# Later weight reloads, float32r filter taps and idle-time transposes at the start of a hybrid encoder block

## The chip, the cores and the metric

The kernel runs on one NeuronCore of a Trainium2 chip. The metric is the device time of one execution in microseconds. The engines are named as the profile names them: PE (matrix multiply) with its weight loads PEld, DVE (VectorE), ACT (ScalarE), POOL (GpSimd) and SP (the queue that issues nearly all DMAs). Each engine runs its own list of instructions in order and waits on semaphores for the others.

## What is computed

One layer of an encoder block, width 2048, 512 tokens, float32 inputs and outputs. Cut to what matters here:

```python
def reference(x, c, w_ada, b_ada, w_in, b_in, ...):
    cond = jax.nn.silu(c)
    mod = (cond @ w_ada[l] + b_ada[l])[:, None, :]
    sh1, sc1, g1, sh2, sc2, g2 = jnp.split(mod, 6, axis=-1)
    h = x * (1.0 + sc1) + sh1
    z = h @ w_in[l] + b_in[l]
    z_u, z_v, z_h, z_g = jnp.split(z, split_pts, axis=-1)
    y_a = spatial_gating(gelu(z_u), gelu(z_v), ...) @ w_branch_a[l]
    y_b = hyena(z_h, ...) @ w_branch_b[l]
    mix = (gate_a * y_a + gate_b * y_b) @ w_o[l] + b_o[l]
    x = layer_norm(ALPHA * x + g1 * mix, ...)
    h = x * (1.0 + sc2) + sh2
    x = layer_norm(ALPHA * x + g2 * (relu(h @ w_m1 + b_m1) ** 2 @ w_m2 + b_m2), ...)

def hyena_filters(L, w1, b1, w2, b2, freq, w3):
    h = jnp.sin(fr * (feats @ w1 + b1))
    h = jnp.sin(fr * (h @ w2 + b2))
    h = h @ w3
    return h.reshape(L, HY_DIRS, HY_ORDER, HY_WIDTH) * window
```

`hyena` convolves its value stream twice with filters of length 512 on both sides; the kernel does this with discrete transforms as matrix products.

## The kernel before

Dense products are made of float32r parts. `split` makes of a float32 tile a high part (an ACT cast, `hi`) and a low part (a DVE subtraction, `lo`); a product is three passes: high by high, high by low, low by high. `dense_steps` makes a group: 512 output columns of one weight matrix for all 512 tokens, in `kp` steps of two input tiles `kc`, with four PSUM banks. One `kp` of a group is 24 matmuls of 128x512 and one weight block.

Weight blocks (128x1024, 512 KB) go through rings of three buffers: `wraw` (as loaded), `whi` and `wlo` (split). The class `Weights` keeps them going: `load` issues the DMA of the next block; `prepare` takes loaded blocks, splits them and calls `load` for each, as long as no more than `ahead` split blocks are waiting; `take`, called by a group, calls `prepare` and hands out a split block. The order of all this is the order in which the program is written: every engine's list and the SP queue follow it.

The start has three parts that matter here.

- **Opening.** Features, `cond` and first modulation tiles are loaded. `Sine` (L283 to L292) runs the filter network: a matmul, a range reduction on DVE, a sine on ACT, twice. The second sine gives the taps' stationary operand in two forms, `even` and `odd` (L361, L362), read with a stride of four.
- **Filter stage.** Eight rounds `n`. A round makes four tap products (`taps`, L385, float32, two passes each) for the next round, one transform of this round's windowed taps (`Forward`, L319 to L331, six float32 products), two modulation sums (`ada_steps(2)`), the window products on DVE (L395) and the transform's sums on DVE (L335 to L339, six operations). Spectra are stored to DRAM.
- **Value groups.** Two dense groups (`two`) run side by side, one `kp` step of each in turn, while the modulated input they read is still being made. An input tile `kc` needs four modulation sums on DVE (L261, `scalar_tensor_tensor` of a 512 KB tile `araw` with `cond`), two small sums on POOL (`mod`, L267, L268), two ACT operations (`act`, L426, and `xT`, L427) and a subtraction on POOL (L428). `ada_steps(4)` does one `kc`. Five `kc` are made in the filter stage; eleven in this stage, at the places that the loop `for kp in range(8)` gives: `weights.prepare()` first, then `ada_steps(4)` until `2 * kp + 2 + LEAD` tiles are there (`LEAD` is 3), then the two groups.

Modulation tiles have three buffers of their own and, while the input tiles are few, up to eight more of the input tiles' own room (`Modulation.load`); a tile is loaded when a sum has freed one. `weights.load()` is called three times at rounds 4 to 6, the first `prepare` at round 6.

After the value groups come about 2550 us of dense groups that this change leaves as they are.

Of the kernel before, what the change touches and what calls it, by code (L numbers as in the profile page):

```python
# [13 lines left out]
AF = mybir.ActivationFunctionType  # L14
# [26 lines left out]
def block_kernel(ctx: ExitStack, tc: tile.TileContext, t):  # L41
# [12 lines left out]
    def slot(name, dt=F32):  # L54
        return heap.tile([P, 512], dt, name=name, tag="slot")

    def slot_pair(name):
        return slot(name + "h", F32R), slot(name + "l", F32R)
# [5 lines left out]
    def bank(name):  # L64
        return psum.tile([P, 512], F32, name=name, tag="bank")

    def f32(ap):
        return ap.bitcast(F32)

    def load(dst, src, queue=nc.sync):  # L70
        queue.dma_start(dst, src)
        return dst

    def split(src, hi, lo):

        nc.scalar.copy(hi, src)  # L76
        nc.vector.tensor_tensor(lo, src, f32(hi), op=OP.subtract)  # L77
# [34 lines left out]
    class Weights:  # L112


        def __init__(self):
            self.blocks = blocks()
            self.raw, self.ready, self.kept, self.used = [], [], {}, set()
            self.ahead, self.done = 1, False

        def load(self):  # L120
            w, cg, kp = next(self.blocks, (None, 0, 0))
# [18 lines left out]
        def prepare(self):  # L140
            for _ in range(4):
                if not self.raw:
                    return
                ring = sum(not self.keeps(r[2]) for r in self.ready)
                if ring > self.ahead and not self.keeps(self.raw[0][1]):
                    return
                raw, what = self.raw.pop(0)
                hi, lo = self.tiles(what)
                split(raw, hi, lo)
                self.ready.append((hi, lo, what))  # L150
                self.load()

        def take(self, w, cg, kp):
            if (w.name, cg, kp) in self.used:
# [58 lines left out]
    def cload(name, shape, queue=nc.sync):  # L213
        return load(const.tile(list(shape), F32, name="c_" + name), t[name], queue)
# [1 line left out]
    warm = small.tile([P, 1], F32, name="warm", tag="warm")  # L216
    nc.vector.memset(warm, 0.0)
    nc.scalar.activation(warm, warm, AF.Sigmoid)
    hw1 = cload("hw1", (EMB, HID), nc.scalar)
    featT = load(slot("featT")[:EMB], t["featT"], nc.scalar)  # L220
    hcol = cload("hcol", (P, 3), nc.scalar)
    hw2 = cload("hw2", (HID, P), nc.scalar)
    cond = const.tile([P, D], F32, name="cond")
    for h in range(4):
        c_ = slice(512 * h, 512 * (h + 1))
        load(cond[:, c_], t["c"][:, c_].broadcast_to([P, 512]))
    inv_d = const.tile([P, 1], F32, name="inv_d")
    nc.vector.memset(inv_d, 1.0 / D)
    sign = const.tile([P, 1], F32, name="sign")
# [4 lines left out]
    nc.gpsimd.memset(first_tap[:, 0:1], 1.0)  # L234
    ident = const.tile([P, P], F32, name="ident")
    make_identity(nc, ident)


    dots = const.tile([P, 6, KC, 2], F32, name="dots")
# [2 lines left out]
    class Modulation:  # L242
# [16 lines left out]
        def step(self):  # L259
            _, raw, m, kc, h = self.raw.pop(0)  # L260
            nc.vector.scalar_tensor_tensor(raw, raw, 1.0, cond[:, 1024 * h:1024 * (h + 1)], op0=OP.mult,  # L261
                                           op1=OP.mult, accum_out=dots[:, m, kc, h:h + 1])
            if len(self.raw) < 10:
                self.load()

    def mod_sum(m, kc, eng=nc.vector):
# [36 lines left out]
    class Forward:  # L303
# [30 lines left out]
        def sums(self, tiles):  # L334
            nc.vector.tensor_tensor(self.ea, self.e0, self.eo, op=OP.add)  # L335
            self.minus(self.e0, self.e0, self.eo)
            for half, e in enumerate((self.ea, self.e0)):
                o = self.o[half]
                nc.vector.tensor_tensor(tiles[half], e, o, op=OP.add)  # L339
                self.minus(tiles[2 + half], e, o)  # L340
# [4 lines left out]
    class Filters:  # L345


        def __init__(self):
            self.one = Sine(hw1, featT, 0, HID)
            self.src, self.raw, self.stores, self.kept, self.win, self.ps = [], [], [], {}, [], []  # L350

        def middle(self):
            x = self.one.reduce()
# [3 lines left out]
        def ready(self):  # L357

            x = self.two.reduce()
            even, odd = slot("a2"), slot("a2")  # L360
            nc.scalar.activation(even, x, AF.Sin)  # L361
            nc.scalar.activation(odd, x, AF.Sin, scale=sign)  # L362
            self.a2 = [a.rearrange("h (p k) -> h k p", k=4) for a in (even, odd)]

        def fetch(self, n):

# [5 lines left out]
            if n in (0, 2):  # L372
                for i in (2, 3) if hf else (0, 1):
                    self.win.append(load(actp.tile([P, 1024], F32, name="win", tag="act"), t["win"][i]))

        def taps(self, n):

            cs = PARTS[n][2]
            if cs == 0:
                self.w = self.raw.pop(0)  # L380
            w, skip = self.w
            for cl in range(4):
                ps = bank("flt")
                extra = cs == 0 and cl == 0
                nc.tensor.matmul(ps, self.a2[cs][:, cl, :], w, start=True, stop=not extra)  # L385
                if extra:
                    nc.tensor.matmul(ps, first_tap, skip, start=False, stop=True)
                self.ps.append(ps)
# [66 lines left out]
    quarters = [cond[:, 512 * h:512 * (h + 1)] for h in range(4)]  # L455
    for s_, c_ in zip(silu, quarters):
        nc.scalar.activation(s_, c_, AF.Sigmoid)
    flt.middle()
    for s_, c_ in zip(silu, quarters):
        nc.vector.tensor_tensor(c_, c_, s_, op=OP.mult)  # L460
# [3 lines left out]
    def x_load():  # L464
        if len(xt) < KC:
            xt.append(load(slot("xT"), t["xT"][len(xt)]))
# [3 lines left out]
    def ada_steps(n):  # L470

        for _ in range(n):
            ada.step()
            done.append(None)
            if len(done) % 4 == 0:
                first_input(len(h1), xt[len(h1)])
                x_load()
# [2 lines left out]
    ada.load()  # L480
    fc = table("fwd", 3)
    for m in (1, 4):
        nc.gpsimd.tensor_scalar(bada[:, m], bada[:, m], 1.0, None, op0=OP.add)
    ada_steps(2)
    flt.ready()
    x_load()
    for _ in range(5):
        ada.load()
    flt.taps(0)
    ada_steps(2)  # L490
    flt.windowed(0)
    for n in range(8):
        if n < 6 and n % 2 == 0:
            flt.fetch(n + 2)
        if n < 7:
            flt.taps(n + 1)
        sums = flt.transform(n)
        ada_steps(2)
        if n < 7:
            flt.windowed(n + 1)  # L500
            flt.store()
        sums()
        if 4 <= n < 7:
            weights.load()
        if n == 6:
            weights.prepare()
    flt.win = []
    windows.clear()
# [3 lines left out]
    two = [dense_steps(ps, t["w_in"], 4 + i, 8, h1) for i, ps in enumerate(ps_v)]  # L512
    yv = []
    for kp in range(8):
        weights.prepare()
        while len(h1) < min(KC, 2 * kp + 2 + LEAD):
            ada_steps(4)
        for i, group in enumerate(two):
            next(group)
            if kp == 7:  # L520
                next(group, None)
                yv.append(short_conv(ps_v[i], 0, i))
        if kp == 1:
            flt.store()
            bin_c = cload("bin", (P, 72))
            hcw = cload("hcw", (P, 24, 4))
            cb = const.tile([P, 24], F32, name="cb")
        if kp == 4:
            nc.vector.tensor_tensor(cb, hcw[:, :, 1], bin_c[:, 16:40], op=OP.mult)
            nc.vector.tensor_tensor(cb, cb, hcw[:, :, 3], op=OP.add)  # L530


    def to_tokens(src, cl, dst):
# [246 lines left out]
    def parts(kc):  # L780
        hi, lo = act_pair(kc)
        split(mix[kc], hi, lo)
        mp.append((hi, lo))
# [343 lines left out]
```

## Time and profile before

| | us |
|---|---|
| median of three runs | 2767.09 |
| lowest, highest run | 2763.63, 2767.69 |
| profiled execution | 2766.04 |
| span of its instructions | 2764.0 |
| PE busy in the span | 2704.5 |
| DVE busy | 1520.6 |
| ACT busy | 770.2 |
| POOL busy | 109.6 |
| mean granted PE clock | 0.992 of full speed |

The span runs from the first to the last instruction; the profiled execution's own time is 2 us longer, for what lies around it. Busy times are sums over the whole span, so they do not say which engine holds a stage up; that is read from single stages. In a timeline a row gives the start, the length, the engine, the line and the operation with its tiles (output, arrow, inputs), how many like it follow each other, and in brackets how long the engine stood idle before it and what ended that. A matmul's record is longer than its distance to the next one, since matmuls overlap; distances are read from starts.

### The profile page before, as it was taken

Reading aid. Unit: us, or ns where it says so; the run is one execution under the profiler, and the core shown is the slowest. Engines: PE = TensorE matmul, PEld = TensorE weight load, DVE = VectorE, ACT = ScalarE, POOL = GpSimd, SP = SyncE. Lnnn points to the kernel's source line nnn. Section 1 sums busy time; section 2 is a strip of 40 time slices with the busy share of each in tenths; the row PEclk is TensorE's granted clock in tenths of the full one; section 3 lists DMA queues with packets and bytes.
Section 4 is the critical chain, followed back from the end, with each engine's and each line's share of the span. In section 5 each row is a group of like instructions: output and inputs, shape, how many; then the busy total and the mean of one; then the engine's idle time right before and its main releaser. Section 6 shows DMA issues by size and latency. Waiting matters only on the chain.

```text
span 2764.0 us, 29765 instructions
## 1 busy us (share of the span) xinstructions
PE 2704.5 (98%) x11917; PEld 2201.6 (80%) x11917; DVE 1520.6 (55%) x2027; ACT 770.2 (28%) x934; POOL 109.6 (4%) x103
## 2 busy tenths in 40 slices
PE   7989999999999999999999999999999999999996
PEld 3667777888888888887988888888888888888885
DVE  7866968644566657536774343343433433434348
ACT  2234322322222222314631221312213122131232
POOL 1120000000000000040020000000000000000001
PEclk9989999999999999999999999999999999999998
DMA  8672332555665558454452323233223233223342
GB/s 328 240 291 77 124 105 99 190 192 190 200 210 191 185 197 294 136 186 163 166 164 96 99 92 102 96 99 97 94 99 97 94 99 100 94 91 105 98 141 74
DMA packets 120474, 400.46 MB, mean 145 GB/s; under 512 B 14219, under 2 KB 14315, under 8 KB 120208
## 3 DMA queue, kind: packets, MB, share of 16 engines
q1 hardware_dynamic: 120024, 398.46, 42.7%
q8 instruction: 93, 1.52, 0.2%
q14 instruction: 45, 0.37, 0.0%
q10 hardware_dynamic: 312, 0.11, 0.0%
HBM read 388.01 MB, written 10.50 MB: 144 GB/s over the span
## 4 chain that ended last, share of the span: by engine, by line
PE 88%; DVE 4%; DMA 2%; issue 1%; ACT 1%; SPq 0%; POOL 0%; DVEq 0%; ACTq 0%
PE d L187 56%; PE t L872 28%; DMA araw<-in_ada 1%; DVE araw L261 1%; DVE wlo L77 1%; PE inv L626 1%; PE inv L614 0%; DMA wraw<-in_w_m 0%; DVE r L993 0%; DVE r L995 0%; DVE r L888 0%; DVE gated L887 0%; DVE st L890 0%; PE tr L537 0%; PE h2T L912 0%
## 5 line engine op out<-in xcount | busy, mean ns | idle before, releaser
L187 PE MATMUL d<-act,whi 128*128 128x512 f32 (+1 forms) x4224 | 1286.9, 387 | 16.2 <-POOL act L428 9.7
L77 DVE TENSOR_TENSOR wlo<-wraw,whi 128x1024 fp32r<-128x1024 f32 x480 | 589.2, 1231 | 1035.2 <-ACT whi L76 1035.1
L187 PEld LDWEIGHTS d<-act,whi 128*128 128x128 f32 x4224 | 788.0, 189 | 181.8 <-POOL act L428 11.3
L76 ACT CAST whi<-wraw 128x1024 fp32r<-128x1024 f32 x480 | 504.4, 1053 | 1534.9 <-PE d L187 914.8
L187 PE MATMUL d<-act,wlo 128*128 128x512 f32 (+1 forms) x2112 | 812.8, 385 | 1.1 <-DVE wlo L77 1.1
L187 PEld LDWEIGHTS d<-act,wlo 128*128 128x128 f32 x2112 | 399.3, 189 | 81.4 <-DVE wlo L77 3.0
L872 PE MATMUL t<-whi,fh 128*128 128x512 f32 x960 | 373.4, 389 | 0.0
L872 PE MATMUL t<-wlo,fh 128*128 128x512 f32 x960 | 373.4, 389 | 0.0
L872 PE MATMUL t<-whi,fl 128*128 128x512 f32 x960 | 373.4, 389 | 0.0
L261 DVE SCALAR_TENSOR_TENSOR araw<-araw,cond 128x1024 f32<-128x1024 f32 x192 | 231.2, 1223 | 9.6 <-DMA araw<-in_ada 9.3
L872 PEld LDWEIGHTS t<-whi,fl 128*128 128x128 f32 x960 | 180.2, 188 | 37.5
L872 PEld LDWEIGHTS t<-whi,fh 128*128 128x128 f32 x960 | 180.2, 188 | 37.4
L872 PEld LDWEIGHTS t<-wlo,fh 128*128 128x128 f32 x960 | 180.2, 188 | 37.4
L872 PE MATMUL t<-whi,act 128*128 128x512 f32 x512 | 160.8, 393 | 0.0
L872 PEld LDWEIGHTS t<-whi,act 128*128 128x128 f32 x512 | 96.9, 189 | 20.2
L887 DVE TENSOR_TENSOR gated<-t,cond 128x512 f32<-128x512 f32 x128 | 87.5, 684 | 31.6 <-PE t L872 31.6
L872 PE MATMUL t<-wlo,act 128*128 128x512 f32 x256 | 100.4, 392 | 2.1 <-DVE wlo L77 2.1
L888 DVE TENSOR_TENSOR r<-r,gated 128x512 f32<-128x512 f32 x128 | 88.6, 692 | 4.4
L187 PE MATMUL d<-whi,act 128*128 128x512 f32 x256 | 78.9, 389 | 0.0
L982 DVE TENSOR_TENSOR relu<-relu 128x512 f32<-128x512 f32 (+1 forms) x68 | 45.6, 671 | 38.2 <-ACT fh L981 38.2
L995 POOL TENSOR_TENSOR r<-r,ln2b 128x512 f32<-128x512 f32 x7 | 11.6, 1662 | 1314.1 <-DVE r L993 1312.8
L872 PEld LDWEIGHTS t<-wlo,act 128*128 128x128 f32 x256 | 48.4, 189 | 12.5 <-DVE wlo L77 2.5
(209 smaller groups left out, 1883.3 us busy)
## 6 DMA issues: line engine op xcount, KB each, us to landing
wraw<-in_w_m SPq DMA_DIRECT2D x264, 512.0 KB, 3.5
araw<-in_ada SPq DMA_DIRECT2D x192, 512.0 KB, 4.9
wraw<-in_w_in SPq DMA_DIRECT2D x144, 512.0 KB, 3.5
wraw<-in_w_o SPq DMA_DIRECT2D x48, 512.0 KB, 3.6
spec<-spec SPq DMA_DIRECT2D x48, 256.0 KB, 3.8
wraw<-in_w_b SPq DMA_DIRECT2D x16, 512.0 KB, 3.5
wraw<-in_w_a SPq DMA_DIRECT2D x16, 512.0 KB, 3.5
xT<-in_xT SPq DMA_DIRECT2D x16, 256.0 KB, 6.4
```

The source lines that it names most:

```text
L76: nc.scalar.copy(hi, src)
L77: nc.vector.tensor_tensor(lo, src, f32(hi), op=OP.subtract)
L187: nc.tensor.matmul(out[i], a, b, start=first and m == 0, stop=last and m == 2)
L261: nc.vector.scalar_tensor_tensor(raw, raw, 1.0, cond[:, 1024 * h:1024 * (h + 1)], op0=OP.mult, op1=OP.mult, accum_out=dots[:, m, kc, h:h + 1])
L626: nc.tensor.matmul(ps[:, cl * P:(cl + 1) * P], conv.y[cl][cs][:, s], ic(4 * cs + COLUMN[cl]), start=(cs == 0), stop=(cs == 1))
L872: nc.tensor.matmul(out[i], a, b, start=kc == 0 and m == 0, stop=kc == 2 * pairs - 1 and m == 2)
L887: nc.vector.tensor_tensor(x, ps[i], g2_row[c], op=OP.mult)
L888: nc.vector.tensor_tensor(r[i][c], r[i][c], x, op=OP.add)
L982: nc.vector.tensor_tensor(x, x, x, op=OP.mult)
L995: eng.tensor_tensor(x, x, ln2_b[c], op=OP.add)
```

## The change

- `Weights.reload` stands where `prepare` called `load`. From before round 0 until after the value groups (`weights.later` is a list) it only notes the load; `weights.flush()`, at the head of each `kp` step, issues what was noted.
- In the `kp` loop one `ada_steps(4)` now comes ahead of `weights.prepare()`, as long as input tiles are missing. The first `prepare` moves from round 6 to round 7.
- Taps: the second sine is written once, split, and its odd form made by two ACT operations on the parts; `parts(n)` splits each `w3` block; a tap is three float32r matmuls instead of one float32 product.
- `busy(n)` issues `n` transposes of the identity into a PSUM bank that nobody reads: 10 between the sines' products, 14 and 14 before the taps.
- The four small loads of the filter network move from the ACT queue to the head of the SP queue, the four loads of `cond` from SP to ACT. The addition of 1 to `bada` moves from POOL to DVE. `step` may load with ten tiles waiting instead of nine.

```diff
@@ class Weights
+        def reload(self):
+            if self.later is None:
+                self.load()
+            else:
+                self.later.append(self.load)
+
+        def flush(self):
+            while self.later:
+                self.later.pop(0)()
...
                 self.ready.append((hi, lo, what))
-                self.load()
+                self.reload()
...
-    hw1 = cload("hw1", (EMB, HID), nc.scalar)
-    featT = load(slot("featT")[:EMB], t["featT"], nc.scalar)
-    hcol = cload("hcol", (P, 3), nc.scalar)
-    hw2 = cload("hw2", (HID, P), nc.scalar)
+    hw1 = cload("hw1", (EMB, HID))
+    featT = load(slot("featT")[:EMB], t["featT"])
+    hcol = cload("hcol", (P, 3))
+    hw2 = cload("hw2", (HID, P))
...
-        load(cond[:, c_], t["c"][:, c_].broadcast_to([P, 512]))
+        load(cond[:, c_], t["c"][:, c_].broadcast_to([P, 512]), nc.scalar)
...
+    def busy(n):
+        ps = bank("busy")
+        for _ in range(n):
+            nc.tensor.transpose(ps[:, :P], ident, ident)
...
-            if len(self.raw) < 10:
+            if len(self.raw) < 11:
                 self.load()
...
-            even, odd = slot("a2"), slot("a2")
-            nc.scalar.activation(even, x, AF.Sin)
-            nc.scalar.activation(odd, x, AF.Sin, scale=sign)
-            self.a2 = [a.rearrange("h (p k) -> h k p", k=4) for a in (even, odd)]
+            nc.scalar.activation(x, x, AF.Sin)
+            even, odd = slot_pair("a2e"), slot_pair("a2o")
+            split(x, *even)
+            for a, b in zip(even, odd):
+                nc.scalar.activation(b, f32(a), AF.Identity, scale=sign)
+            self.a2 = [[a.rearrange("h (p k) -> h k p", k=4) for a in pair] for pair in (even, odd)]
...
+        def parts(self, n):
+            if PARTS[n][2] == 0:
+                w, skip = self.raw.pop(0)
+                both = slot_pair("w3")
+                split(w, *both)
+                self.w.append((*both, skip))
...
-            w, skip = self.w
+            wh, wl, skip = self.w[0] if cs == 0 else self.w.pop(0)
+            ah, al = self.a2[cs]
...
-                nc.tensor.matmul(ps, self.a2[cs][:, cl, :], w, start=True, stop=not extra)
+                for m, (a, w) in enumerate(((ah, wh), (ah, wl), (al, wh))):
+                    nc.tensor.matmul(ps, a[:, cl, :], w, start=m == 0, stop=m == 2 and not extra)
...
     for s_, c_ in zip(silu, quarters):
         nc.scalar.activation(s_, c_, AF.Sigmoid)
+    busy(10)
     flt.middle()
...
     for m in (1, 4):
-        nc.gpsimd.tensor_scalar(bada[:, m], bada[:, m], 1.0, None, op0=OP.add)
+        nc.vector.tensor_scalar(bada[:, m], bada[:, m], 1.0, None, op0=OP.add)
+    busy(14)
     ada_steps(2)
     flt.ready()
+    flt.parts(0)
+    busy(14)
...
     flt.windowed(0)
+    weights.later = []
     for n in range(8):
...
+        if n < 6:
+            flt.parts(n + 2)
         sums()
         if 4 <= n < 7:
             weights.load()
-        if n == 6:
+        if n == 7:
             weights.prepare()
...
     for kp in range(8):
+        weights.flush()
+        if len(h1) < KC:
+            ada_steps(4)
         weights.prepare()
         while len(h1) < min(KC, 2 * kp + 2 + LEAD):
             ada_steps(4)
...
+    weights.flush()
+    weights.later = None
```

How the order of instructions moves is shown at three places. First DVE from the last sums of the filter stage into the value groups, before (`wlo` is the low part of a weight block, `araw` a modulation tile):

```order
L339 TENSOR_TENSOR spec<-bf_e_626,f_o 128x512
L313 SCALAR_TENSOR_TENSOR spec<-bf_e_626,f_o 128x512
L77 TENSOR_TENSOR wlo<-wraw,whi 128x1024 x3
L261 SCALAR_TENSOR_TENSOR araw,dots<-araw,cond 128x1024 x8
L77 TENSOR_TENSOR wlo<-wraw,whi 128x1024 x2
L261 SCALAR_TENSOR_TENSOR araw,dots<-araw,cond 128x1024 x8
```

and with the change:

```order
L356 TENSOR_TENSOR spec<-bf_e_740,f_o 128x512
L330 SCALAR_TENSOR_TENSOR spec<-bf_e_740,f_o 128x512
L77 TENSOR_TENSOR wlo<-wraw,whi 128x1024 x2
L278 SCALAR_TENSOR_TENSOR araw,dots<-araw,cond 128x1024 x4
L77 TENSOR_TENSOR wlo<-wraw,whi 128x1024 x2
L278 SCALAR_TENSOR_TENSOR araw,dots<-araw,cond 128x1024 x4
L77 TENSOR_TENSOR wlo<-wraw,whi 128x1024 x2
L278 SCALAR_TENSOR_TENSOR araw,dots<-araw,cond 128x1024 x4
L77 TENSOR_TENSOR wlo<-wraw,whi 128x1024
L278 SCALAR_TENSOR_TENSOR araw,dots<-araw,cond 128x1024 x4
L77 TENSOR_TENSOR wlo<-wraw,whi 128x1024
```

Eight sums and two splits in turn have become four sums and, from the fourth turn on, one split. Before, two further splits stood ahead of the last round's sums.

Second ACT at the same place, before (two input tiles, then two casts):

```order
L426 ACTIVATE act_858<-xT,mod 128x512
L427 ACTIVATE xT<-xT,mod 128x512
L426 ACTIVATE act_878<-xT,mod 128x512
L427 ACTIVATE xT<-xT,mod 128x512
L76 CAST whi<-wraw 128x1024 x2
```

and with the change:

```order
L452 ACTIVATE act_978<-xT,mod 128x512
L453 ACTIVATE xT<-xT,mod 128x512
L76 CAST whi<-wraw 128x1024
L452 ACTIVATE act_1002<-xT,mod 128x512
L453 ACTIVATE xT<-xT,mod 128x512
L76 CAST whi<-wraw 128x1024
```

Each cast now stands behind the two operations of one input tile instead of a pair of casts behind those of two.

Third ACT between the second sine's product and the first modulated input tile, before:

```order
L284 ACTIVATE sine<-flt,hfb,c_hcol 128x512
L361 ACTIVATE a_181<-sine 128x512
L362 ACTIVATE a_182<-sine,sign 128x512
L426 ACTIVATE act_214<-xT,mod 128x512
L427 ACTIVATE xT<-xT,mod 128x512
```

and with the change:

```order
L301 ACTIVATE sine<-flt,hfb,c_hcol 128x512
L377 ACTIVATE sine<-sine 128x512
L76 CAST a2eh<-sine 128x512
L381 ACTIVATE a2oh<-a2eh,sign 128x512
L381 ACTIVATE a2ol<-a2el,sign 128x512
L76 CAST w3h<-w_124 128x512
L452 ACTIVATE act_272<-xT,mod 128x512
```

The first tap, which waited for the first of two operations, now waits for the last of five.

## Rows read from the trace of the kernel before

**Rows 1.** Stages: span, busy us (count) by engine, PEclk, DMA share, GB/s.
```profile
20.00:98.00 78.00, 77.76 (x169) 39.40 (x170) 68.14 (x111) 13.58 (x20) 6.68 (x12) 1.00 0.71 263
98.00:213.00 115.00, 100.05 (x384) 78.01 (x383) 82.66 (x123) 41.45 (x51) 30.62 (x36) 0.90 0.78 285
213.00:2764.00 2551.00, 2522.70 (x11364) 2083.43 (x11362) 1357.76 (x1772) 707.70 (x854) 65.94 (x43) 1.00 0.40 134
```

**Rows 2.** Timeline of DVE, value groups: the splits of two turns.
```profile
124.45 2.62 DVE L77 TENSOR_TENSOR wlo<-wraw,whi 128x1024 fp32r<-128x1024 f32 x2 [4.25 <-ACT whi L76]
...
140.45 2.61 DVE L77 TENSOR_TENSOR wlo<-wraw,whi 128x1024 fp32r<-128x1024 f32 x2 [4.22 <-ACT whi L76]
```

**Rows 3.** Timeline of the last input tile's turn, all engines.
```profile
192.62 1.21 DVE L261 SCALAR_TENSOR_TENSOR araw<-araw,cond 128x1024 f32<-128x1024 f32 x1
...
193.76 1.22 DVE L261 SCALAR_TENSOR_TENSOR araw<-araw,cond 128x1024 f32<-128x1024 f32 x1
...
198.79 1.23 DVE L261 SCALAR_TENSOR_TENSOR araw<-araw,cond 128x1024 f32<-128x1024 f32 x1 [2.66 <-DMA araw<-in_ada]
...
200.11 0.20 POOL L267 TENSOR_TENSOR mod<-dots 128x2 f32<-128x2 f32 x1 [9.63 <-DVE araw L261]
...
202.18 1.98 ACT L76 CAST whi<-wraw 128x1024 fp32r<-128x1024 f32 x2
...
203.25 1.46 DVE L77 TENSOR_TENSOR wlo<-wraw,whi 128x1024 fp32r<-128x1024 f32 x1 [3.22 <-ACT whi L76]
...
203.68 0.50 PE L187 MATMUL d<-act,whi 128*128 128x512 f32 x1 [1.70 <-POOL act L428]
```

**Rows 4.** Timeline of PE, value groups without waits.
```profile
108.06 0.62 PE L187 MATMUL d<-act,whi 128*128 128x512 f32 x2
...
112.14 0.62 PE L187 MATMUL d<-act,whi 128*128 128x512 f32 x2
```

**Rows 5.** Stretches of the start, columns as in rows 1.
```profile
80.00:97.00 17.00, 17.00 (x41) 8.38 (x41) 15.54 (x24) 5.17 (x7) 1.27 (x1) 1.00 0.03 7
...
205.00:210.00 5.00, 5.00 (x17) 3.95 (x16) 4.89 (x7) 5.00 (x9) 0.00 (x0) 0.67 0.59 210
```

**Rows 6.** Timeline of PE, filter stage: one transform matmul two rounds apart, one round's taps.
```profile
41.89 1.02 PE L319 MATMUL f_ee<-flt,fwd 128*128 128x512 f32 x2
...
47.04 3.60 PE L385 MATMUL flt<-w,a 128*128 128x512 f32 x8
...
60.43 1.02 PE L319 MATMUL f_ee<-flt,fwd 128*128 128x512 f32 x2
```

**Rows 7.** Weight loads by line and form: count, busy us, mean ns, idle before.
```profile
L187 PEld LDWEIGHTS d<-act,whi 128*128 128x128 f32 x4224 | 788.0, 189 | 181.8 <-POOL act L428 11.3 <-issue 7.7 <-ACT act L426 6.6
...
L385 PEld LDWEIGHTS flt<-w,a 128*128 128x128 f32 x64 | 19.4, 311 | 20.0 <-ACT a L361 7.6 <-issue 4.8 <-DVE spec L315 2.3
...
L537 PEld LDWEIGHTS tr<-ident,hy 128*128 128x128 f32 x64 | 9.0, 208 | 1.0 <-issue 0.5
```

**Rows 8.** Timeline of PE: transposes of a later stage.
```profile
224.24 1.11 PE L537 MATMUL tr<-ident,hy 128*128 128x128 f32 x8
```

**Rows 9.** Timeline of the opening, PE and ACT.
```profile
5.13 1.93 PE L283 MATMUL flt<-featT,c_hw 33*64 33x512 f32 x2 [5.13 <-DMA featT<-in_featT]
...
19.56 0.63 ACT L361 ACTIVATE a<-sine 128x512 f32<-128x512 f32 x1 [4.57 <-DVE sine L292]
...
20.24 2.09 PE L385 MATMUL flt<-w,a 128*128 128x512 f32 x2 [6.07 <-ACT a L361]
...
24.27 7.83 PE L385 MATMUL flt<-w,a 128*128 128x512 f32 x14
```

**Rows 10.** Timeline of DVE, end of the filter stage and first value step.
```profile
102.38 1.22 DVE L77 TENSOR_TENSOR wlo<-wraw,whi 128x1024 fp32r<-128x1024 f32 x1
...
109.81 1.23 DVE L77 TENSOR_TENSOR wlo<-wraw,whi 128x1024 fp32r<-128x1024 f32 x1 [4.21 <-ACT whi L76]
110.95 1.22 DVE L261 SCALAR_TENSOR_TENSOR araw<-araw,cond 128x1024 f32<-128x1024 f32 x1
```

More of the change, by code (lines that the diff above doesn't have):

```diff
@@ L117, in __init__ @@
             self.raw, self.ready, self.kept, self.used = [], [], {}, set()
-            self.ahead, self.done = 1, False
+            self.ahead, self.done, self.later = 1, False, None
+        def reload(self):
[6 more added lines that the diff above has]
+                self.later.pop(0)()
         def load(self):
@@ L349, in __init__ @@
             self.one = Sine(hw1, featT, 0, HID)
-            self.src, self.raw, self.stores, self.kept, self.win, self.ps = [], [], [], {}, [], []
+            self.src, self.raw, self.stores, self.kept, self.win, self.ps, self.w = [], [], [], {}, [], [], []
         def middle(self):
@@ L374, in fetch @@
                     self.win.append(load(actp.tile([P, 1024], F32, name="win", tag="act"), t["win"][i]))
+        def parts(self, n):
[4 more added lines that the diff above has]
+                self.w.append((*both, skip))
         def taps(self, n):
             cs = PARTS[n][2]
-            if cs == 0:
-                self.w = self.raw.pop(0)
-            w, skip = self.w
+            wh, wl, skip = self.w[0] if cs == 0 else self.w.pop(0)
+            ah, al = self.a2[cs]
             for cl in range(4):
```

## The prediction

> **What bounds the kernel now.** I read the stages first, then the timelines of single engines, then the waits. In the stage table [rows 1] TensorE (PE) is busy for 2522.7 of the 2551 us after 213 us, and for all of the filter stage (20 to 98). It loses time in one place that this change touches: from 98 to 213 it is busy 100 of 115 us, at a mean granted clock of 0.90. That is the stage of the two value groups. Nothing after it is changed, so the question is when this stage ends.
>
> The stage is not held by PE. VectorE (DVE) runs a loop there: eight modulation sums (two input tiles `kc`), then two low halves of weight blocks (`wlo`), and again. Each time it stands idle for 4.2 us before the first `wlo`, waiting for ScalarE's (ACT's) cast `whi`, and the loop comes back after 140.45 - 124.45 = 16.0 us [rows 2]. ACT itself waits: its queue has the cast behind the two `act` operations of the input tile just summed. One such turn in full [rows 3]: the last sum starts at 198.79, GpSimd's `mod` sum at 200.11, the cast at 202.18, `wlo` at 203.25, that is 4.46 us from the last sum's start to `wlo`. PE needs 10.9 us for the 48 matmuls of a turn (18 of them in 112.14 - 108.06 us, 0.227 each [rows 4]), so it waits, and in such stretches its clock falls to the lower level (0.67 on average from 205 to 210 [rows 5]).
>
> **The filter stage, step by step.** One round of it is four tap products and one transform; the same transform matmul returns after two rounds, at 41.89 and 60.43: 18.54 us a pair [rows 6], all PE. A tap is now two passes of 0.43 us (8 in 3.60, [rows 6]) and becomes three float32r products. Their price is that of the dense loop, 0.227 us, if the strided load of the stationary operand stays hidden: it takes 311 ns where the dense loop's contiguous one takes 189 [rows 7]. Since a matmul can start before the record of its load ends (eight transposes stand in 1.11 us, one every 0.12 [rows 8], with strided loads of 208 ns [rows 7]), I take 0.23. The other end is 311 + 38 = 0.35, the load with the margin that the dense loop leaves (227 - 189). So a round saves 4 x (0.86 - 0.69) = 0.67 and a pair 1.34; at worst a pair costs 4 x (1.05 - 0.86) x 2 = 1.5. DVE gets one more subtraction a pair; it is busy 68 of 78 us in that stage [rows 1], so that is covered. Three pairs follow round 0: **-4.0 us**, bounds -4.4 and +4.5.
>
> The Trainium skill, "TensorE: Matmul & The Clock Gate", section "LDWEIGHTS (loading the stationary operand)", makes the load a matter of columns alone (about 107 ns for 128), whatever the stride. The two load rows [rows 7] differ by 122 ns at equal columns, so the trace speaks against it; by it the load would certainly hide.
>
> Round 0 comes out even. The first product now can start earlier, because the features lead the SP queue instead of the ACT queue beside four loads of `cond`; it waited for them until 5.13 [rows 9]. I take 1 us, between none and 2. But between the second sine and the first tap ACT has four operations more (cast, two sign products, cast of `w3`), near 0.6 us each (the sign product took 0.63 [rows 9]): +2.5, so the first tap moves from 20.24 to 21.7. From there the passes run at the lower clock, 1.03 us each at 20.24, until a little over 27 us (14 passes in 7.83, a mix [rows 9]). Before: 13.4 us of PE work at the high clock (18 tap and 12 transform passes at 0.43, and 0.5 of gaps) from 20.24, half speed to 27.4, gives 37.2. Now 24 x 0.23 + 14 x 0.43 + 0.5 = 12.0 from 22.4 (the low half of `w3` comes last): 36.9. **0**, bounds -2 if the clock were high from the first tap, +2 if it rose one such stretch later. The 38 transposes of `busy` take 0.12 us each at the high clock [rows 8] and 0.24 at the low one, so the 28 ahead of the taps last 6.7 us at most; PE waits 6.07 us for its first tap there [rows 9], and that wait grows by 1.5, so they are free; the ten ahead of the second sine stand in a wait of the same kind. What they can change is the clock. I take no gain from them because near 2 us of idle time remain between the last transpose and the first tap, and an idle time of 1.70 us [rows 3] was followed by the lower level [rows 5].
>
> Here a page speaks against the change: the Trainium skill, "TensorE: Matmul & The Clock Gate", Part 4, says that the high clock does not engage for transposes. No row of this trace shows transposes alone; by the page the sum stays as it is, and if it is wrong here the sum is 2 us better.
>
> **The value groups.** DVE finishes the last transform's sums and two `wlo` at 102.38 [rows 10]. In the change two `wlo` stand behind these sums instead of ahead of them: same count, same moment, less the 4.0: 98.4. PE waits some 3 us there for the first `wlo`; it has slack. Then the difference in order decides. Before, the next thing was a third `wlo`, whose buffer PE freed late, so the first sum started at 110.95 [rows 10]. Now four sums come first, at **98.4**: 12.5 us ahead.
>
> But each `kc` is now followed by its own `wlo`, whose cast stands on ACT behind that `kc`'s `act`. So the idle time comes once per `kc` instead of once per two: three sum pitches of 1.15 (192.62 to 193.76 [rows 3]), 4.46, and 1.14 for the `wlo` (109.81 to 110.95 [rows 10]) make **9.05 us a kc, 18.1 a pair, against 16.0**. From `kc` 5 to `kc` 15 that is ten times 9.05 and two further `wlo` (2.3): 92.8. The last `kc` starts at 191.2, before at 192.62 [rows 3]: the lead is used up. Its last tile is loaded only after its first sum in both kernels, so its `wlo` follows 203.25 - 192.62 = 10.63 later, at 201.8, ready at 203.0.
>
> Now the end. Before, at 203.68 [rows 3], PE had 35 matmuls of the groups left: 7.9 us, and 1.7 lost at the lower clock (0.33 of 5 us [rows 5]): 213.3. Now both blocks of the last step come behind the last `kc`: 48 matmuls, 10.9 us, from 203.0, and the same 1.7: 215.6. **+2.3 us** on the profiled execution, 2766.04 to 2768.3; that execution lies 1.05 under the median of the runs shown, so on the median 2767.09 + 2.3 = **2769.4**.
>
> The reloads themselves cost nothing. SP stood behind `wlo` with a reload whose raw buffer was not yet free, which left the transfers almost idle from 80 to 97 us (share 0.03 [rows 5]); issued a step later they no longer hold the modulation tiles up. But DVE waited for a tile only 2.66 us at the end [rows 3]; the queue was not the bound, so freeing it is worth 0 to 2.7.
>
> **Rivals.**
> - Faster, the loads bind: transfers took 0.78 of the stage [rows 1], after a hole of 17 us [rows 5]. If the loop's 16 us came from them, the groups would run at PE's pace, 16 x 5.45 = 87 us from 97: 184 instead of 213, -29 us, 2738. Against it: DVE's idle rows name the cast, not a tile [rows 2]. 0.04.
> - Faster, the interleaving costs less than I think: 16.0 a pair stays and the lead of 12.5 us remains, less 2.9 for the 13 matmuls that now come behind the last `kc`: -9.6, 2757.5. For it: ACT has nothing else to do. Against it: the cast is queued behind `act`. 0.09.
> - Slower, the clock becomes the bound: PE now works 5.45 us and waits 3.6, again and again, where it waited some 2 us in 16 before. It decides when the lower level lasts through a block: at half the clock a block takes twice 5.45 = 10.9 us, more than the 9.05 of the loop. Priced at the two last blocks low throughout: 21.8 instead of 10.9 + 1.7 = 12.6, so 9.2 beside the 2.3: +11.5, 2778.6. 0.19.
> - Slower, the strided load shows: taps at 0.35 us, +4.5 instead of -4.0, so 8.5 beside the 2.3: +10.8, 2777.9. 0.08.
> - That the change does not move what it says is excluded by the order lists.
>
> **How the numbers follow.** About 0.2% (5.5 us) can be told from no change. The forecast with its own spread (round 0 by 2 either way, the last tile's wait by 2.7 less, the clock by 1.7 either way: 2763 to 2773) has 0.60, nearly all of it inside 0.2%. Faster: 0.04 + 0.09 + 0.02 of the forecast's edge. Slower: 0.19 + 0.08 and 0.02 of its edge. So 0.15, 0.56, 0.29. The range takes in both slower cases and reaches down to 2758: what is left out is the first rival, most of the second, and a clock low for longer.
>
> **What would show it.** In the new profile: pairs of rounds 17.2 us apart; the first modulation sum of the stage near 98.4; DVE idle 3.2 to 3.3 us before nearly every `wlo`, released by `whi`, eleven times; `kc` steps 9.05 apart; PE idle in pieces of 3 to 4 us from about 150 us on; the last `wlo` pair near 203. I am wrong if the `kc` step is well under 9 us, if PE runs without gaps through the stage, or if tap matmuls come slower than one in 0.25 us.

## The result and the profile after

The changed kernel takes 2773.61 us (median of 13 runs, 2770.64 to 2774.97); the kernel before, on the same chips, 2766.13 (median of 13). The ratio is 1.0027, with a 95% interval of 1.0018 to 1.0035: slower by 7.5 us. The range of 2758 to 2779 holds it, but the likeliest case, +2.3 us and hardly to be told from no change, was 5 us too kind. The profiled execution took 2774.97 us, its span 2773.3; it was the slowest of the thirteen, 1.4 us above their median, and the marks below are its own.

First the stages, with the columns of [rows 1]:

```profile
20.00:98.00 78.00, 75.20 (x211) 45.28 (x209) 70.91 (x119) 16.07 (x25) 7.06 (x14) 0.93 0.72 266
98.00:213.00 115.00, 94.43 (x347) 71.85 (x348) 76.42 (x112) 35.06 (x41) 19.71 (x34) 0.89 0.77 275
213.00:2764.00 2551.00, 2531.73 (x11400) 2090.74 (x11398) 1359.15 (x1774) 712.69 (x862) 64.07 (x42) 1.00 0.40 134
```

Between 98 and 213 us TensorE does 347 products instead of 384 [rows 1]. The missing 37 come later; behind them the two kernels run alike.

DVE in the stage of the value groups (start, length, operation, and in brackets the idle time before it and what ended that):

```profile
102.83 1.22 DVE L278 SCALAR_TENSOR_TENSOR araw<-araw,cond 128x1024 f32<-128x1024 f32 x1
...
131.59 1.49 DVE L77 TENSOR_TENSOR wlo<-wraw,whi 128x1024 fp32r<-128x1024 f32 x1 [3.22 <-ACT whi L76]
...
140.88 1.49 DVE L77 TENSOR_TENSOR wlo<-wraw,whi 128x1024 fp32r<-128x1024 f32 x1 [3.22 <-ACT whi L76]
...
198.17 1.21 DVE L278 SCALAR_TENSOR_TENSOR araw<-araw,cond 128x1024 f32<-128x1024 f32 x1
...
204.16 1.23 DVE L278 SCALAR_TENSOR_TENSOR araw<-araw,cond 128x1024 f32<-128x1024 f32 x1 [2.47 <-DMA araw<-in_ada]
...
208.60 3.73 DVE L77 TENSOR_TENSOR wlo<-wraw,whi 128x1024 fp32r<-128x1024 f32 x3 [3.21 <-ACT whi L76]
```

The splits stand 140.88 - 131.59 = 9.29 us apart, one input tile each, with 3.22 us of waiting for the cast in every turn. Over the stage (from 102 to 212 us) that wait adds up as follows in the kernel before (total, times, longest):

```profile
DVE wlo L77 <- ACT whi L76: 28.3, 8, 4.3
```

and in the changed one, in shorter pieces but more of them:

```profile
DVE wlo L77 <- ACT whi L76: 35.4, 11, 3.2
```

One such turn of the changed kernel, ACT, GpSimd, DVE and PE:

```profile
147.53 0.81 ACT L452 ACTIVATE act<-xT,mod 128x512 fp32r<-128x512 f32 x1 [6.68 <-POOL mod L285]
148.38 0.81 ACT L453 ACTIVATE xT<-xT,mod 128x512 f32<-128x512 f32 x1
149.09 1.03 ACT L76 CAST whi<-wraw 128x1024 fp32r<-128x1024 f32 x1
149.26 1.26 POOL L454 TENSOR_TENSOR act<-xT,act 128x512 fp32r<-128x512 f32 x1 [1.77 <-ACT xT L453]
150.16 1.46 DVE L77 TENSOR_TENSOR wlo<-wraw,whi 128x1024 fp32r<-128x1024 f32 x1 [3.21 <-ACT whi L76]
150.18 0.50 PEld L198 LDWEIGHTS d<-act,whi 128*128 128x128 f32 x2 [2.90 <-ACT whi L76]
150.18 1.22 PE L198 MATMUL d<-act,whi 128*128 128x512 f32 x2 [2.48 <-ACT whi L76]
```

The cast needs nothing from this tile: it stands on ACT behind `act` and `xT`, which wait 6.68 us for the sums. TensorE then waits for the cast as well. The split takes 1.46 us instead of 1.22: GpSimd is still busy with L454 when it starts, which the experiments come back to.

The opening on PE, with some of the later `f_ee` rows, which begin a transform (from 44.78 to 62.08 and from 62.08 to 79.40 is a pair of rounds each):

```profile
14.03 2.07 PE L300 MATMUL flt<-sine,c_hw 64*128 64x512 f32 x2 [5.06 <-ACT sine L371]
16.03 5.18 PE L253 MATMUL busy<-ident 128*128 128x128 f32 x28
23.83 0.81 PE L411 MATMUL flt<-w3h,a2eh 128*128 128x512 f32 x1 [2.62 <-ACT w3h L76]
...
35.43 1.02 PE L336 MATMUL f_ee<-flt,fwd 128*128 128x512 f32 x2
...
44.78 1.02 PE L336 MATMUL f_ee<-flt,fwd 128*128 128x512 f32 x2
...
62.08 1.02 PE L336 MATMUL f_ee<-flt,fwd 128*128 128x512 f32 x2
...
70.05 1.02 PE L336 MATMUL f_ee<-flt,fwd 128*128 128x512 f32 x2
...
79.40 1.02 PE L336 MATMUL f_ee<-flt,fwd 128*128 128x512 f32 x2
```

The first tap comes at 23.83 (before 20.24 [rows 9]), the first transform 3.5 us later than before (31.94 there), and a pair of rounds takes 62.08 - 44.78 = 17.30 us against 18.54 [rows 6]. The granted clock of the same stretch, four microseconds a row:

```profile
20.00:24.00 4.00, 1.38 (x12) 1.14 (x10) 1.32 (x4) 3.15 (x5) 0.00 (x0) 0.92 1.02 400
24.00:28.00 4.00, 4.00 (x6) 1.45 (x7) 2.95 (x6) 0.62 (x1) 0.39 (x2) 0.50 1.03 410
28.00:32.00 4.00, 4.00 (x10) 3.17 (x11) 1.92 (x4) 1.01 (x2) 1.28 (x1) 0.50 1.04 405
32.00:36.00 4.00, 4.00 (x14) 3.33 (x14) 4.00 (x7) 0.00 (x0) 0.00 (x0) 0.80 1.03 411
```

The transposes went from one every 0.21 us to one every 0.11 at about 20 us: the clock was up while nothing but transposes ran. Then PE idled 2.62 us, and the taps, mostly 0.43 us a pass, ran at the lower level until 33.5. The column for the granted clock stands at 1.00 up to the first change on record, in the kernel before too, where loads of the first taps stand 0.86 us apart up to 27.0 and 0.43 behind that. So a first rise is read here from such distances.

### The profile page after: what moved, and what is told of

Read it like the earlier page. It is cut to its first block, busy times and chain, and to the rows that moved or that the text cites. A ratio compares the mean times of both kernels' runs of the same rounds, so it can differ in the third digit from the quotient of the medians.

```text
span 2773.3 us, 29922 instructions
## 1 busy us (share of the span) xinstructions
PE 2711.6 (98%) x11987; PEld 2214.6 (80%) x11987; DVE 1523.4 (55%) x2034; ACT 773.2 (28%) x940; POOL 93.6 (3%) x101
## 4 chain that ended last, share of the span: by engine, by line
PE 87%; DVE 4%; DMA 1%; ACT 1%; issue 1%; POOL 0%; SPq 0%; DVEq 0%; ACTq 0%; POOLq 0%
PE d L198 56%; PE t L910 28%; PE inv L664 1%; PE inv L652 0%; DVE wlo L77 0%; DMA wraw<-in_w_m 0%; DVE r L1031 0%; DVE r L1033 0%; DMA araw<-in_ada 0%; DVE r L926 0%; DVE araw L278 0%; DVE gated L925 0%; DVE st L928 0%; PE tr L575 0%; PE h2T L950 0%
```

## The experiments

The marks that the runs were read by, in us from the start of each profiled span; "end" is the first product behind the two groups, and "sums" are the stage's first modulation sum and the first one of the last input tile:

| kernel | 1st transform | 1st group product | sums | end | median |
|---|---|---|---|---|---|
| before | 31.9 | 97.5 | 110.9, 192.6 | 213.3 | 2766.1 |
| the change | 35.4 | 100.2 | 102.8, 198.2 | 222.3 | 2773.6 |
| b_taps | 33.2 | 95.0 | 108.5, 189.8 | 210.5 | 2763.5 |
| b_value | 33.8 | 101.6 | 104.3, 199.6 | 223.8 | 2775.9 |
| a_noextra | 34.4 | 99.1 | 115.0, 195.6 | 213.8 | 2767.2 |
| a_castfirst | 34.4 | 99.1 | 101.8, 173.0 | 203.4 | 2756.2 |
| a_nobusy | 34.6 | 99.3 | 102.0, 197.3 | 221.4 | 2774.4 |
| a_busymore | 33.0 | 97.7 | 100.4, 195.7 | 220.0 | 2772.1 |
| a_oldloads | 35.2 | 100.0 | 102.6, 198.0 | 220.3 | 2773.5 |
| best | 29.5 | 91.3 | 97.8, 165.9 | 199.0 | 2751.7 |
| best_nobusy | 32.8 | 94.6 | 100.2, 167.6 | 199.3 | 2752.6 |
| best2 | 29.4 | 92.1 | 98.7, 163.0 | 195.2 | 2747.7 |

**The value-group part alone (b_value).** The kernel before with `Weights.reload` and `flush` and these edits:

```diff
-            if len(self.raw) < 10:
+            if len(self.raw) < 11:
...
-                self.load()
+                self.reload()
...
+    weights.later = []
...
-        if n == 6:
+        if n == 7:
             weights.prepare()
...
     for kp in range(8):
+        weights.flush()
+        if len(h1) < KC:
+            ada_steps(4)
         weights.prepare()
```

> The kernel before with the value-group part of the change alone (loads noted and issued a step later, one turn of sums ahead of the splits, first splits in round 7). Theory A (each split waits for its cast behind act, 3.2 us, eleven times, and a split behind idle time costs 1.39): first sum of the stage near 102.4, 9.3 us an input tile, last tile's first sum near 197.7, stage ends near 221.5: 2773. Theory B (the loss is in the opening, lower clock and late condition vector; the loop is worth +2.3): 2768.5.

It took 2775.89 us, ratio 1.0034 (1.0021 to 1.0048): 9.6 us slower, more than the whole change. Its profiled execution was the slowest of five (2778.16), and 1.9 us of that one's loss come from the opening, which has no edit (the clock rose at 30.8 us instead of 27.4). Theory A holds: the loss is in the value groups.

**The taps alone (b_taps).** The kernel before with `parts`, the split second sine and three float32r products a tap.

> The kernel before with the float32r taps alone. Theory A (a pair of rounds is held by VectorE at 17.3 us and no longer by TensorE at 18.54; the four added operations move the first tap by 2.5 us): rounds 17.3 us a pair, first tap near 22.8, the groups' first product near 95 instead of 97.45, and as the loop of the groups hangs on the blocks that TensorE frees, the same 2 to 3 us less at the end: 2763.5. Theory B (the filter stage gives nothing back, because the loop of the groups waits for its casts anyway): 2766.

2763.47 us, ratio 0.9994 (0.9985 to 1.0003): 2.3 us less, in the direction of theory A and of the size it gives, though the interval includes no change. With b_value's +9.6 it makes +7.3, about the whole change (+7.5). A pair of rounds takes 17.30 us here as in the changed kernel, where one looks like this (columns as in [rows 1]):

```profile
62.08:79.40 17.32, 17.32 (x52) 10.72 (x50) 17.25 (x30) 3.21 (x5) 1.66 (x3) 1.00 0.91 321
```

and one of the kernel before:

```profile
41.89:60.43 18.54, 18.54 (x43) 9.71 (x42) 17.07 (x29) 2.70 (x4) 1.67 (x3) 1.00 0.78 277
```

DVE is now busy for 17.25 of 17.32 us, and theory A took it for the new bound. TensorE's rows speak against that part of A. The round from 62.08 to 70.05 takes 7.97 us, and twelve transform passes of 0.43 and twelve tap passes of 0.235 make just that, with no room for a wait. The round with the extra one-row product takes 1.4 us more, as it does in the kernel before. So TensorE still sets the pace, and the 1.24 us saved are its own. DVE has no idle time left and falls behind a little: the first of its transform's sums (L352) returns after 17.38 us (65.01 to 82.39).

**Without the extra turn of sums (a_noextra).**

```diff
     for kp in range(8):
         weights.flush()
-        if len(h1) < KC:
-            ada_steps(4)
         weights.prepare()
```

> The change without the turn of sums ahead of the splits: loads still noted and issued a step later. Theory A (a turn of four sums with a split of its own costs 9.27 us, a turn of eight with two splits 16.0): three further splits stand ahead of the first sum again, the last waits for the second block that TensorE frees, first sum near 115.4 (before 110.95), then 16.0 a pair, last tile's first sum near 197, its two splits near 207.6, 35 products left, stage ends near 217.8: 2770.6. Theory B (the order of sums and splits does not matter, the late issue of the loads does): 2773.6 or more.

2767.22 us, 1.0005 (0.9996 to 1.0014): 6.4 us under the change, twice what A expected; so B is not the whole cause. The loop is back at two tiles in 16.0 us, with one wait of 4.2:

```profile
128.45 2.62 DVE L77 TENSOR_TENSOR wlo<-wraw,whi 128x1024 fp32r<-128x1024 f32 x2 [4.25 <-ACT whi L76]
...
144.44 2.61 DVE L77 TENSOR_TENSOR wlo<-wraw,whi 128x1024 fp32r<-128x1024 f32 x2 [4.21 <-ACT whi L76]
```

The first sum came where A put it (115.0), the end 4 us earlier than A said: TensorE's clock stayed high from 196 us on, and the wait for the last tile was 1.7 us instead of 2.7.

The turn is not all of the loss. This kernel is still 3.8 us behind b_taps (2767.22 against 2763.47), whose loop has the same 16.0 us. Of that 1.2 us are there at the first transform; the stage's first sum comes 6.4 us later (115.0 against 108.5), with all five first splits ahead of it, two of which b_taps has made earlier. The later first `prepare` and the later reloads move together here, and no run separates them.

**Casts ahead of the sums (a_castfirst).** The wait itself is taken away, with the number of the sums kept; a turn of four sums and one split now stands ahead of each group's step:

```diff
-                split(raw, hi, lo)
+                nc.scalar.copy(hi, raw)
+                if between:
+                    between()
+                    between = None
+                nc.vector.tensor_tensor(lo, raw, f32(hi), op=OP.subtract)
...
-        if len(h1) < KC:
-            ada_steps(4)
-        weights.prepare()
-        while len(h1) < min(KC, 2 * kp + 2 + LEAD):
-            ada_steps(4)
         for i, group in enumerate(two):
+            had = len(h1)
+            weights.prepare((lambda: ada_steps(4)) if had < KC else None)
+            if had == len(h1) < KC:
+                ada_steps(4)
             next(group)
```

> The change with each cast of a weight block written ahead of the four sums of its turn and the subtraction behind them, one turn ahead of each group's step. Theory A (the wait for the cast behind act is what holds the loop): no idle time of 3.2 us ahead of the splits, 5.7 to 7 us an input tile, TensorE works through the groups with few gaps and ends them near 192 instead of 222: 2743 to 2750. Theory B (the loads hold the stage at the 285 GB/s that it moved on average, 2.75 MB an input tile, 9.6 us): VectorE waits for tiles instead, 2773 as in the change.

2756.16 us, 0.9962 (0.9949 to 0.9974): 17.5 us under the change and 10 under the kernel before. The idle times ahead of the splits are gone while sums remain, and a turn takes 113.19 - 106.37 = 6.8 us instead of 9.3:

```profile
106.37 1.22 DVE L164 TENSOR_TENSOR wlo<-wraw,whi 128x1024 fp32r<-128x1024 f32 x1
...
110.94 2.31 DVE L282 SCALAR_TENSOR_TENSOR araw<-araw,cond 128x1024 f32<-128x1024 f32 x1
...
113.19 1.22 DVE L164 TENSOR_TENSOR wlo<-wraw,whi 128x1024 fp32r<-128x1024 f32 x1
```

Two stretches of the same kernel, with the columns of [rows 1]:

```profile
110.00:130.00 20.00, 20.00 (x90) 16.57 (x89) 20.00 (x26) 7.34 (x9) 11.34 (x9) 1.00 1.03 408
130.00:150.00 20.00, 16.89 (x72) 12.90 (x71) 18.85 (x26) 6.97 (x9) 8.99 (x9) 1.00 1.01 381
```

So theory A is right on the cause; but the groups ended at 203.4, not 192. DVE is now busy for all of the first stretch, and one sum of four takes 2.31 us instead of 1.22 there. The transfers are busy throughout at 381 to 408 GB/s, and DVE waits 6.5 us in all for late tiles.

**The transposes (a_nobusy, a_busymore).** In the change, the three calls of `busy` taken out; and the last 14 transposes made 38, so that they reach up to the first tap.

> The change without its 38 transposes. Theory A (transposes raised the granted clock at 20.0 us, 2.6 us of idle time then dropped it at 23.4, and the taps ran at the lower level until 33.6): without them the clock rises once, some 7 us after the first tap as before (20.24 to 27.4), that is near 31; first transform done near 39 instead of 40.17, 1 to 2 us faster, 2772. Theory B (the transposes do nothing to the clock, the late rise comes from the late taps): clock and time as in the change, 2773.6.

> The last 14 transposes become 38, so that TensorE has no idle time left ahead of the first tap (24 more at 0.11 us against a gap of 2.8). Theory A: the clock that rose at 20.0 stays high through the taps, the 12.0 us of work of round 0 run from 23.8 at the high level, first transform done near 36 instead of 40.17: 4 us faster, 2769.5. Theory B (transposes count for nothing): the clock rises as late as before, 2773.6.

Without them 2774.37 us (1.0029, 1.0018 to 1.0041), against 1.0027 for the change: no difference can be seen, where A expected 1 to 2 us less. In that profile the clock rose at 32.0 and the first transform came at 34.6. With 38 of them 2772.12 us (1.0021, 1.0012 to 1.0029), 1.5 us under the change, with intervals that overlap; the first transform came 2.5 us earlier, A expected 4. The stretches of the second kernel:

```profile
20.00:24.00 4.00, 4.00 (x35) 3.79 (x33) 1.35 (x3) 3.15 (x5) 0.00 (x0) 1.00 1.03 404
24.00:28.00 4.00, 3.89 (x10) 2.29 (x10) 3.45 (x7) 0.76 (x1) 0.40 (x2) 0.84 1.03 410
28.00:32.00 4.00, 4.00 (x14) 3.52 (x13) 2.85 (x4) 0.87 (x2) 1.29 (x1) 0.73 1.04 404
```

The clock rose at 19.9 and was high when the taps began, but it dropped once more, from 26.7 to 30.1, although there was no gap of microseconds before. The first taps are thin work (24.00 to 28.00: ten products, some of them one row deep), but that this dropped it is argued, not shown; in `best`, below, the same first taps behind 1.44 us of idle time did not drop it.

**The first loads (a_oldloads).** The four small loads back on ACT's queue, `cond` on SP's.

> The change with its first loads as before (small loads of the filter network on ACT's queue, cond on SP's). Theory A (cond's fourth quarter landed only at 11.40 us from ACT's queue, its sigmoid held ACT's first sine from 11.43 to 13.35): the first sine is back near 11.4 and the first tap comes at 21.9 instead of 23.83; the taps run at the lower level there, so half of it or all of it counts, 1 to 2 us faster, 2771.6 to 2772.6. Theory B (the new order of loads gains its 0.4 us on the first product and costs nothing else): 2773.6 to 2774.

2773.51 us (1.0024, 1.0014 to 1.0034): theory B, no difference. ACT in the change shows why A looked likely:

```profile
11.40 0.63 ACT L483 ACTIVATE silu<-cond 128x512 f32<-128x512 f32 x1 [2.39 <-DMA cond<-in_c]
12.05 1.28 ACT L371 ACT_TABLE_LOAD   x1
13.35 0.63 ACT L371 ACTIVATE sine<-sine 64x512 f32<-64x512 f32 x1
...
20.51 0.63 ACT L377 ACTIVATE sine<-sine 128x512 f32<-128x512 f32 x1 [3.59 <-DVE sine L309]
21.17 0.62 ACT L76 CAST a2eh<-sine 128x512 fp32r<-128x512 f32 x1
...
23.18 0.60 ACT L76 CAST w3h<-w 128x512 fp32r<-128x512 f32 x1
```

In the profile with the old loads the first sine was 1.3 us earlier (12.01), but the second only 0.2 (20.30): DVE reduces the second product behind two modulation sums, and these began at 14.47 instead of 13.46, since the first product, with its later features, had come at 5.72 instead of 4.71. From the second sine to the first tap the chain is 3.3 us in both kernels, and of the 3.6 us that the tap is later than in the kernel before it is 2.6.

**Everything together (best, best_nobusy, best2).** `best` adds to a_castfirst: the old first loads, `flt.parts(0)` ahead of `flt.ready()`, 20 transposes last, and

```diff
+        if n == 7:
+            weights.flush()
...
-        if n == 7:
+        if n == 6:
             weights.prepare()
...
+        if kp == 7:
+            flt.store()
         if kp == 1:
-            flt.store()
```

> Cast ahead of the sums (as in a_castfirst), with the first loads as before, the split of w3 ahead of the second sine's reduction, 20 transposes instead of the last 14, the first two blocks split in round 6 and their reloads issued at the head of round 7, and the eight late stores of spectra moved behind the groups. Theory A (in a_castfirst the loads bound the stage from 110 us on, at 400 GB/s, after a hole from 94 to 101, and 2 MB of stores stood among them): first tap near 21.3, first product of the groups near 95, fewer waits for tiles, groups end near 192 instead of 203: 2745. Theory B (the loop is bound elsewhere, by VectorE's 5.7 us a turn or by TensorE): no better than 2753.

2751.66 us, 0.9950 (0.9938 to 0.9963). The first product of the groups came earlier than expected (91.3), the end later (199.0 instead of 192): both theories have a part, since a turn still takes 6.8 us. Then the same without its transposes:

> The fastest kernel so far (best) without its 44 transposes. Theory A (transposes raise the granted clock and keep it, where they end 1.4 us ahead of the first tap instead of 2.8): the clock rises only some 7 us after the first tap, near 29 to 31 instead of 18.9; the 12 us of work of round 0 take 3 to 4 us more, first transform starts near 33 instead of 29.5: 3 to 4 us slower, 2755. Theory B (transposes do nothing): as with them, 2751.7.

2752.62 us, 0.9949 (0.9935 to 0.9963): the same time. The first part of A held, the clock rose at 30.5 instead of 18.9 and the first transform came 3.3 us later; but the end moved by 0.3. The wait that takes it up, in `best`:

```profile
173.52 1.23 DVE L282 SCALAR_TENSOR_TENSOR araw<-araw,cond 128x1024 f32<-128x1024 f32 x1 [2.64 <-DMA araw<-in_ada]
```

Without the transposes DVE reaches this tile later and waits 1.57 us for it, and the sum starts at 173.79: the tile lands at nearly the same time in both, and what the opening gains is waited away there. The turn's length remained. In `best`, DVE and GpSimd at one turn:

```profile
112.60 1.21 DVE L282 SCALAR_TENSOR_TENSOR araw<-araw,cond 128x1024 f32<-128x1024 f32 x1
113.35 1.61 POOL L458 TENSOR_TENSOR act<-xT,act 128x512 fp32r<-128x512 f32 x1 [1.78 <-ACT xT L457]
...
113.74 2.30 DVE L282 SCALAR_TENSOR_TENSOR araw<-araw,cond 128x1024 f32<-128x1024 f32 x1
```

The sum that starts during GpSimd's subtraction ends 1.1 us after it (116.04 against 114.96), as if it began only then. `best2` gives that subtraction to DVE:

```diff
-        nc.gpsimd.tensor_tensor(lo, xt, f32(hi), op=OP.subtract)
+        late.append(lambda: nc.vector.tensor_tensor(lo, xt, f32(hi), op=OP.subtract))
```

with the entries of `late` issued behind the next turn's split (the four first tiles keep GpSimd).

> best with the subtraction of the input tiles (act low part, 1.28 us on GpSimd) moved to VectorE, behind the next turn's sums, for the tiles of the value groups. Theory A (a sum that starts beside that GpSimd operation takes 2.30 instead of 1.21 us, once per input tile, and this makes a turn 6.8 us instead of 5.7): all sums take 1.21, the subtraction costs 0.6 to 0.7 of VectorE's time, a turn takes 6.3 to 6.4 us unless the loads (0.92 to 0.96 busy in best) then bind, groups end 3 to 5 us earlier: 2747 to 2749. Theory B (a sum of 2.30 us has another cause, a late tile or cast): the long sums stay, a turn takes 7.4, 2758.

2747.70 us, 0.9930 (0.9918 to 0.9943): 18.5 us under the kernel before, 4 under `best`, as A said. The sums all take 1.22, and a turn is 117.08 - 110.75 = 6.3 us:

```profile
110.75 0.68 DVE L458 TENSOR_TENSOR act<-xT,act 128x512 fp32r<-128x512 f32 x1
...
114.79 1.22 DVE L282 SCALAR_TENSOR_TENSOR araw<-araw,cond 128x1024 f32<-128x1024 f32 x1
...
117.08 0.68 DVE L458 TENSOR_TENSOR act<-xT,act 128x512 fp32r<-128x512 f32 x1
```

## Why the prediction was right in kind and short by 5 us

- **The bound.** That the loop of sums and splits on DVE, and not PE, sets the end of the value groups is shown from both sides: taking the cast's wait away gained 17.5 us (a_castfirst), and taking the extra turn out gained 6.4 (a_noextra).
- **One wait per tile.** The mechanism was as forecast: eleven waits of 3.2 us, 9.3 us a tile. The step "9.05 us a kc" was mis-sized by the last of its three numbers: a split behind an idle time takes 1.39 us to the next sum, not 1.14. The sign was in [rows 3], where the split behind the wait has 1.46 us; 1.14 came from a row of [rows 10] with no GpSimd operation beside it. Ten turns and 0.33 us for two small operations that I left out make 95.3 us instead of 92.8: 2.5 us.
- **The filter stage.** "A pair 1.34 less" came out at 18.54 - 17.30 = 1.24, and the strided load does not show (taps 0.235 us apart; the section that the prediction names there speaks of columns, and "whatever the stride" is the prediction's own reading). The missing 0.1 is the pass of 0.235 us where 0.23 was taken. But "DVE ... is covered" failed: TensorE did not have to wait for DVE, but DVE had no idle time left, and its sums and splits around the last transform ended 0.64 us later behind the transform's start than before (102.83 - 92.51 against 102.38 - 92.70). Together 1.0 us of the expected 4.0 were missing.
- **Round 0.** "It comes out even" failed: the first transform came 3.5 us later. The chain from the second sine to the first tap grew from 0.68 to 3.3 us, about as costed; the second sine before it came 0.95 us later (20.51 against 19.56 [rows 9]) where I had counted on 1 us earlier, as the gain of the features was lost behind `cond` and the sums. And the clock, for which I had taken the rise of before (27.4), came back only at 33.5. My upper bound for this step was +2. As the rise lay between 27.4 and 33.5 in kernels whose opening differs little (27.4 in before, 30.8 in b_value with the same opening), this term should have had a range of some 3 us.
- **The sum.** 3.5 + 1.0 + 2.5 make 7.0, of which the end gives back 0.3: the groups' end stands at 222.3 where 215.6 was forecast. On medians 7.5 was measured where 2.3 was forecast. The marks are those of the slowest execution: a_oldloads, with the same median and its last tile begun at 198.0, ended its groups at 220.3, so the stretch behind the last tile varies by 2 us between executions. It is also in part luck that the range holds 2773.6: the forecast's own spread ended at 2773, and the room above it was made for the lower clock and the strided load, neither of which came.
- **The rivals.** Faster because the loads bind: not here; once the cast's wait is gone, DVE does wait for tiles (6.5 us in a_castfirst). The interleaving costing less: no. The lower clock through whole blocks: TensorE lost some 0.1 of its clock in the stage, as before (0.89 against 0.90 [rows 1]), so no. The last tile was still waited for, 2.47 us against 2.66 [rows 3].
- **The reloads.** "No longer hold the modulation tiles up" failed. SP no longer stands with a reload, but it stands as long with the load of a modulation tile, for whose buffer it waits 17.6 us; before, the longest wait of this kind was 22.7 us for a split. The transfers stand still all the same, now from 84 to 97 us. And "cost nothing" is not shown: 3.8 us between a_noextra and b_taps lie in the later reloads, the later first splits and the opening together. SP's queue and the transfers in the changed kernel (second row with the columns of [rows 1]):

```profile
78.96 18.33 SPq L71 DMA_DIRECT2D araw<-in_ada  x2
...
84.00:97.00 13.00, 13.00 (x37) 7.45 (x36) 12.97 (x23) 1.17 (x2) 0.01 (x1) 1.00 0.00 1
```

## What to carry to other kernels

Where a split has a cast on one engine and a subtraction on another, the cast's place in its queue counts: put it ahead of work that waits, or every turn pays the whole chain from sum to cast. Splitting a turn in two to have results earlier doubles the number of such waits, and the lead that it buys is spent after a fixed number of turns. An opening that is made faster counts only if nothing later waits it away, as the last tile's load does in `best`.

## What was not expected of the hardware

GpSimd and VectorE hold each other up. A sum on DVE that starts during GpSimd's subtraction of 128x512 takes 2.2 to 2.3 us instead of 1.21, in nine of the eleven turns of `best`, and with the subtraction on DVE none does. The 1.46 us of a split in the changed kernel fit the same: GpSimd's row ends at 150.52 and the split 1.1 us later. By this the mis-sized number of the forecast, 1.39 instead of 1.14 us, comes from GpSimd; the subtraction was not moved in that kernel, so there it is argued. The Trainium skill, "SBUF — State Buffer", section "Who interferes with whom", says that a VectorE instruction with two inputs in SBUF and a GpSimd instruction that reads SBUF share a port as a lock, where whichever starts first makes the other wait; the trace agrees, by 1.1 us a sum.

Transposes do count for the clock, read from the distances of products: with them it rose at 18.3 to 20.0 us, during a run of nothing else, and without them at 30.5 and 32.0. The Trainium skill, "TensorE: Matmul & The Clock Gate", Part 4, says that the high clock does not engage for them; on this point the measurement decides. The earlier rise is worth up to 3.3 us at the first transform and 0.3 at the end of the groups in `best`; in the change, taking the transposes out or adding 24 moved the median by 0.8 and 1.5 us, within the intervals.
